# Layer 1's state space steps spread evenly over grouped-query attention in a two-layer hybrid diffusion step

## The chip, the core and the metric

The kernel runs on one core of a Trainium2 chip. The metric is the time of one execution on the device, in microseconds (us); the figure for the kernel before is the median of three runs, 1797.16 us (1796.97 to 1809.3).

## The reference

Two layers of a backbone over 128 prompt tokens and 512 latent tokens, width 1024. Each layer computes, cut to what matters here:

```python
h = layer_norm(x) * (1.0 + sc1) + sh1
z = h @ lp['w_in']
u, q_na, k_na, v_na, q_g, k_g, v_g = jnp.split(z, cuts, axis=-1)
ssm_out, st = ssm_mixer(u, lp, h0_f, h0_b)          # S5: complex diagonal, both directions, then gelu and a gate
na_out  = na_latent(q_na, k_na, v_na, ck, cv, bias)  # 4 heads, 8x16 windows; dense for the prompt
gqa_out = attend_dense(q_g, k_all, v_all)            # 8 query heads on 2 key heads
o = concat([ssm_out, na_out, gqa_out]) @ lp['w_out']
x = layer_norm(ALPHA * x + g1 * o, ...)
```

followed by a SwiGLU feed-forward part. The three mixers read different slices of `z` and do not depend on one another; only `w_out` reads all three. Everything is float32.

## The kernel before

The 640 tokens are five tiles of 128, the first of them the prompt. A product with a weight matrix is split into a high and a low half and takes three matmuls (`mm3`, L311 to L313): high by high, low by high, high by low. The halves of a weight come from a cast on ACT (L283) and a subtraction on POOL or DVE (L284).

A scheduler of the tile framework sets the order on each engine. It takes the program as it is written and weighs it with priorities; units of attention stand under a high priority (`PRIO` = 300), so that what is written between them, the state space steps among it, fills behind them. Each engine then runs its own list strictly in that order. PSUM comes from three pools of two buffers each: `psM` (weights' products, L714, L724, the transposes of L808, the gate of L825), `psT` (transposes and the second products of attention), `psS` (scores, and the second products of the state space model, L767 and L770). Loads and stores are issued by SP, in one list.

`layer` runs, per layer:

1. GQA: keys and values, then 18 units (`pipelined`, one unit ahead). A unit's scores are L1157, its exponentials L1163, its second product L1184. After each unit `between(n)` writes some steps of other work: steps of the state space generator by the table `SSMN`, and by `WINN` pieces of the `w_in` product that neighbourhood attention needs (L311 to L313 with 128x320 results; L1265 copies a piece out of PSUM and L1266 stores it to the scratch `zqk`).
2. NA (neighbourhood attention): two head pairs of five units, one for the prompt and four for the latent tiles. `na_prep` loads `zqk` (L876) and casts it (ACT L877, L878, L283; DVE L879, L284); the prompt's scores are L916; a latent unit's front is L942, L943, L947 into `psS`, then DVE L948 with ACT L950, DVE's maximum L952, ACT's exponentials L955; its back transposes (L859), copies out (ACT L290 or DVE L288), multiplies (L978), divides by the sums (L853, ACT L982, DVE L983) and splits the result (ACT L283, DVE L284). Two fronts run ahead of a back (`DEPTH` = 2). `na_prep` of the second pair is written ahead of its sixth unit (`PREP1`). After the backs, `SSMC` = (1, 2, 0, 2, 1, 0, 1, 0, 2, 1) writes state space steps that are left.
3. `wout`: the product with `w_out`, then the feed-forward part. Its first matmul in layer 1 starts at 1237.04 us.

The state space generator (`ssm`, L671) has 17 steps over eight pairs of groups. Step 1 loads u and writes pair 0's front: loads of four tables (L697, L698, L699, L709) and four matmuls (L714). Step 2p+2 is pair p's turn (four transposes, L724), the next pair's front, and pair p's rotation on DVE (L732 to L753, with a scan in L742). Step 2p+3 is pair p's back (L767, L770, copied out by ACT, L772). Step 17 is the last back and the tail: the state out (L793 to L799), two gelus on ACT (L802, with a table load ahead), 16 transposes (L808), the gate (L825, tanh L827) and the split.

In layer 1 before, 11 of the 17 steps stand in GQA (its eighth to seventeenth units) and six in NA, the tail among them after the back of NA's fifth unit.

Of the kernel before, what the change touches and what calls it, by code (L numbers as in the profile page):

```python
# [157 lines left out]
class Build:  # L158
# [2 lines left out]
    SIZES = dict(b5=1280, xs=640, ys=768, k4=1024, ev=512, zt=512)  # L161
    BUFS = dict(b5=6, xs=8, ys=4, k4=10, ev=4, zt=2)
    TILES = (2, 1, 4, 3, 0)
    SSMN = (0, 0, 0, 0, 0, 0, 0, 1, 1, 1, 1, 1, 1, 1, 1, 1, 2, 0)
    WINN = (2, 0, 1, 1, 2, 0, 1, 1, 1, 1, 1, 1, 1, 1, 1, 1, 0, 2)
    ADAN = (0,) * 6 + (1,) * 6 + (0,) * 6
    FILA = (2, 3, 2, 2, 2)
# [1190 lines left out]
    def layer(self, l, A, xsrc, T, nxt, tab, todo):  # L1358

        nc, I = self.nc, self.I  # L1360
        V, S, G = nc.vector, nc.scalar, nc.gpsimd
        M, zkv = A["M"], A["zkv"]
        hh, hl = A["h"]
        zq, sss, put_q = A["zq"], A["sss"], A["put_q"]
        znv = self.dp.tile([NT, 128, 256], F32, name=self.nm("znv"))
        zu = self.dp.tile([256, NTOK], F32, name=self.nm("zu"))
        zqk = [self.dp.tile([2, 128, NTOK], F32, name=self.nm("zqk")) for _ in range(2)]
        mixd = self.dp.tile([4, 128, NTOK], F32, name=self.nm("mixd"))

        def put_v(i, t, ps):  # L1370
            nc.sync.dma_start(znv[i], t)
            if i == 0:
                nc.sync.dma_start(self.O["na_v"][l], t)

        def tiles(piece, put, order=range(NT)):
            w = self.win_w(l, piece)
            for i in order:
                yield self.win_tile(w, i, hh, hl, put)

        def features(piece, put):  # L1380
            w = self.win_w(l, piece)
            for m in range(2):
                for b in range(2):
                    yield self.win_T(w, m, b, hh, hl, put)

        def chain(*gens):
            for g in gens:
                yield from g

        K = self.gqa_kv(l, zkv)  # L1390
        for _ in features(0, self.put_u(zu)):
            pass
        mx = []

        def mixed(k):

            if not mx:
                mx.extend(self.newh())
            return mx[0][:, k], mx[1][:, k]

        ssm = self.ssm(l, zu, T, mixed)
        fill = chain(tiles(6, put_q(1)), tiles(3, put_v), features(1, self.put_qk(l, 0, zqk[0])),
                     features(2, self.put_qk(l, 1, zqk[1])))
        for _ in range(self.FILL0[l]):
            next(fill, None)
        for _ in range(self.TAB1):
            next(tab, None)
        units, preps = [], []
        for kv in range(2):
            u, prep = self.gqa_units(l, kv, zq[kv], K, sss[kv], mixd)  # L1410
            units += u
            preps += [(prep, a[2][0]) for a in u]

        def between(n):
            for _ in range(self.TABN[n]):
                next(tab, None)
            for _ in range(self.SSMN[n]):
                next(ssm, None)
            for _ in range(self.WINN[n]):
                next(fill, None)  # L1420
            for _ in range(self.ADAN[n]):
                if todo:
                    self.ada(l, M, *todo.pop(0))
            if n + self.AHEAD < len(units):
                with self.tc.high_priority(self.PRIO):
                    preps[n + self.AHEAD][0](preps[n + self.AHEAD][1])

        self.pipelined(units, 1, between)
        for _ in fill:
            pass  # L1430
        Ns = [self.na_prep(l, 0, zqk[0], znv)]

        def gqa_out(k):
            t = self.k4()[:, 0:SLAB]
            nc.sync.dma_start(t, mixd[k])
            self.split(t, *mixed(4 + k), V if self.MIXE[k] else G)

        units = self.na_units(l, Ns[0], *mixed(2))
        live, n, depth = {}, 0, self.DEPTH
        for n in range(10 + depth):  # L1440
            if n == self.PREP1:
                Ns.append(self.na_prep(l, 1, zqk[1], znv))
                units = units + self.na_units(l, Ns[1], *mixed(3))
            if n < 10:
                with self.tc.high_priority(self.PRIO):
                    live[n] = units[n][0](units[n][2])
            for k in range(4):
                if self.MIX[k] == n:
                    gqa_out(k)
            if n >= depth:  # L1450
                with self.tc.high_priority(self.PRIO):
                    units[n - depth][1](units[n - depth][2], live.pop(n - depth))
                for _ in range(self.SSMC[n - depth]):
                    next(ssm, None)
        for _ in ssm:
            pass
        return self.wout(l, M, mx, xsrc, nxt)
# [457 lines left out]
```

## Time and profile before

| | us |
|---|---|
| median of three runs | 1797.16 |
| lowest, highest | 1796.97, 1809.3 |
| the profiled execution | 1788.01 |
| its span in the trace | 1786.0 |
| layer 1, GQA's first scores (L1157) | from 1041.35 |
| layer 1, NA's first scores (L916) | from 1183.93 |
| layer 1, first matmul of `w_out` | from 1237.04 |

The profiled execution is one of its own and took 9.2 us less than the median. Its span leaves out 2.0 us around the program. PE is TensorE, PEld its weight loads, DVE VectorE, ACT ScalarE, POOL GpSimd, SP the engine that issues DMAs. Mean granted TensorE clock over the span is 0.96 of full speed; in a stretch of it that reads 1.0 the clock is at 2.4 GHz, at 0.5 it is at 1.2 GHz, and between them it was at each for a part.

### The profile page before, as it was taken

The page shows a single profiled execution, that of the slowest core. Times are in us where ns is not written, and L with a number is a line of the kernel's source. Part 1 is how long each engine was busy: PE and PEld are TensorE (multiplying, and loading weights), DVE is VectorE, ACT ScalarE, POOL GpSimd, SP SyncE. Part 2 cuts the span into 40 slices and gives each one's busy share as a digit, 9 for nine tenths or more (in the row PEclk, how much of TensorE's full clock was granted, in tenths as well). Part 3 has the DMA queues.
Part 4 walks back from the last instruction along what each step waited for, and adds up shares of the span by engine and source line. Part 5 has one row for each costly group of instructions (what it writes and reads, how often), then busy time and mean ns, then how long its engine had stood idle before and what let it go on. Part 6 is the DMA issues. An engine that isn't in the chain of part 4 may idle for free. (4 is left out here: it accounts for less than half of the span.)

```text
span 1786.0 us, 31489 instructions
## 1 busy us (share of the span) xinstructions
PE 1641.2 (92%) x11624; PEld 1435.8 (80%) x11624; DVE 1222.5 (68%) x2460; ACT 827.3 (46%) x1800; POOL 763.5 (43%) x651
## 2 busy tenths in 40 slices
PE   5899899898899999999897989998979999999997
PEld 2898677676788888798796978876859899998995
DVE  5765546627678776778877565565487687876777
ACT  5444446657443334243345556665574242433433
POOL 3853203059235343346266232111785254454463
PEclk9999899798999999999999999998989999999999
DMA  9445767446353645232324243463542231222212
GB/s 335 112 126 139 238 194 213 123 158 203 107 172 122 195 127 182 81 121 71 121 85 157 92 129 96 111 187 115 180 148 85 94 107 59 92 74 69 98 62 81
DMA packets 183114, 234.90 MB, mean 132 GB/s; under 512 B 78960, under 2 KB 112048, under 8 KB 182960
## 3 DMA queue, kind: packets, MB, share of 16 engines
q1 hardware_dynamic: 182960, 232.88, 42.3%
q8 instruction: 92, 1.51, 0.3%
q14 instruction: 62, 0.51, 0.1%
HBM read 203.57 MB, written 29.39 MB: 130 GB/s over the span
## 5 line engine op out<-in xcount | busy, mean ns | idle before, releaser
L284 POOL TENSOR_TENSOR wl<-wr,wh 128x512 fp32r<-128x512 f32 x362 | 504.2, 1413 | 522.8 <-ACT wh L283 343.2
L283 ACT CAST wh<-wr 128x512 fp32r<-128x512 f32 x450 | 275.2, 619 | 383.9 <-DVE wr L1597 88.6
L311 PE MATMUL psM<-hh,wh 128*128 128x320 f32 x560 | 180.3, 322 | 2.3 <-DVE ys L1647 1.1
L313 PE MATMUL psM<-hh,wl 128*128 128x320 f32 x560 | 177.9, 318 | 0.0
L312 PE MATMUL psM<-hl,wh 128*128 128x320 f32 x560 | 177.8, 318 | 0.0
L311 PEld LDWEIGHTS psM<-hh,wh 128*128 128x128 f32 x560 | 108.5, 194 | 6.2 <-issue 1.8
L311 PE MATMUL psT<-hh,wh 128*128 128x320 f32 x352 | 109.9, 312 | 0.0
L313 PEld LDWEIGHTS psM<-hh,wl 128*128 128x128 f32 x560 | 108.6, 194 | 1.5 <-issue 1.4
L312 PE MATMUL psT<-hl,wh 128*128 128x320 f32 x352 | 109.2, 310 | 0.0
L313 PE MATMUL psT<-hh,wl 128*128 128x320 f32 x352 | 109.0, 310 | 0.0
L312 PEld LDWEIGHTS psM<-hl,wh 128*128 128x128 f32 x560 | 108.7, 194 | 0.3
L230 POOL TENSOR_TENSOR sm<-sm,mhalf 128x1 f32<-128x1 f32 (+2 forms) x46 | 54.3, 1182 | 92.3 <-DVE sm L260 49.3
L1647 DVE TENSOR_TENSOR ys<-ys,psM 128x320 f32<-128x320 f32 x140 | 65.0, 481 | 33.8 <-PE psM L313 31.9
L1160 DVE TENSOR_REDUCE psS<-psS 128x1 f32<-128x640 f32 x64 | 52.7, 828 | 47.4 <-PE psS L1157 45.6
L1647 DVE TENSOR_TENSOR ys<-ys,psT 128x320 f32<-128x320 f32 x140 | 65.0, 481 | 28.8 <-PE psT L313 27.7
L311 PE MATMUL psT<-b,wh 128*128 128x320 f32 x240 | 76.5, 319 | 8.3 <-DVE ys L1647 7.4
L311 PE MATMUL psM<-b,wh 128*128 128x320 f32 x240 | 76.1, 317 | 5.8 <-DVE ys L1647 5.8
L284 POOL TENSOR_TENSOR wl<-ws,wh 128x512 fp32r<-128x512 f32 x40 | 53.6, 1340 | 64.4 <-ACT wh L283 62.6
L859 PE MATMUL psT<-ident,ys 128*128 128x128 f32 x440 | 73.2, 285 | 5.8 <-DVE hl L284 3.3
L311 PE MATMUL psM<-wh,xs 128*128 128x512 f32 x190 | 74.9, 394 | 3.7 <-DVE k L1771 3.5
L311 PE MATMUL psT<-wh,xs 128*128 128x512 f32 x190 | 75.6, 398 | 2.9 <-DVE k L1771 2.9
L1597 DVE TENSOR_TENSOR ws<-wr,wr 128x512 f32<-128x512 f32 x40 | 37.0, 926 | 58.9 <-DMA wr<-in_w_ffn_in_dram 28.3
(440 smaller groups left out, 4907.9 us busy)
## 6 DMA issues: line engine op xcount, KB each, us to landing
wr<-in_w_ffn_in_dram SPq DMA_DIRECT2D x88, 512.0 KB, 3.7
ev<-in_w_ada_dram SPq DMA_DIRECT2D x112, 256.0 KB, 4.0
wr<-in_w_ffn_out_dram SPq DMA_DIRECT2D x40, 512.0 KB, 3.9
wr<-in_w_out_dram SPq DMA_DIRECT2D x32, 512.0 KB, 3.6
wr<-in_w_in_dram SPq DMA_DIRECT2D x28, 512.0 KB, 4.8
wa<-in_w_ada_dram SPq DMA_DIRECT2D x24, 512.0 KB, 4.7
k<-in_x_dram SPq DMA_DIRECT2D x10, 512.0 KB, 5.6
xs<-zqk SPq DMA_DIRECT2D x32, 160.0 KB, 3.7
```

The source lines that it names most:

```text
L230: self.nc.gpsimd.tensor_tensor(out=o, in0=v, in1=self.mhalf.broadcast_to([128, v.shape[1]]), op=ALU.pow)
L283: nc.scalar.copy(hi, src)
L284: (lo_eng or nc.vector).tensor_tensor(out=lo, in0=src, in1=hi.bitcast(F32), op=ALU.subtract)
L311: nc.tensor.matmul(ps, lhsT=ah, rhs=bh, start=first, stop=False)
L312: nc.tensor.matmul(ps, lhsT=ah, rhs=bl, start=False, stop=False)
L313: nc.tensor.matmul(ps, lhsT=al, rhs=bh, start=False, stop=last)
L859: self.nc.tensor.transpose(pt[:, j * 128:(j + 1) * 128], s, self.ident)
L1160: V.tensor_reduce(out=m, in_=sp[:, :, 0:320], axis=AX.XY, op=ALU.max, negate=True)
L1597: V.tensor_tensor(out=o, in0=x, in1=y, op=op)
L1647: V.tensor_tensor(out=o, in0=x, in1=y, op=ALU.add)
```

## The change

The table of steps becomes one row per layer. Layer 0 keeps its row. In layer 1, one step stands after each of the third to seventeenth units, so 15 of 17 steps are written in GQA and two are left for NA: the last pair's turn and rotation stand there after the first back, and the last back with the tail after the second.

```diff
-    SSMN = (0, 0, 0, 0, 0, 0, 0, 1, 1, 1, 1, 1, 1, 1, 1, 1, 2, 0)
+    SSMN = ((0,) * 7 + (1,) * 9 + (2, 0), (0, 0) + (1,) * 15 + (0,))
...
         def between(n):
...
-            for _ in range(self.SSMN[n]):
+            for _ in range(self.SSMN[l][n]):
                 next(ssm, None)
```

No instruction is added or taken away; they move from layer 1's third GQA unit on, up to the start of `w_out`. Three places:

PE where NA begins, before: the back of pair 4 (L767, L770), the last two matmuls of `w_in` (L312, L313), a transpose of `na_prep`, the turn of pair 5 (L724), and the first latent scores (L942).

```order
L767 MATMUL psS_2426_13203<-k4_2386_12942,k4_2387_12943 80x128 x7
L770 MATMUL psS_2426_13203<-k4_2385_12941,k4_2230_12112 80x128 x2
L312 MATMUL psM_2430_13230<-hl_1952_10410,wh_2369_12850 128x320
L313 MATMUL psM_2430_13230<-hh_1951_10409,wl_2370_12851 128x320
L859 MATMUL psT_2443_13293<-ident_84,ev_2440_13286 128x128 x2
L724 MATMUL psM_2462_13368<-ident_84,k4_2424_13173 128x80 x4
L942 MATMUL psS_2453_13320<-b5_2433_13259,b5_2432_13258 128x256
```

PE at the same place, with the change: the back there is pair 6's.

```order
L770 MATMUL psS_2438_13303<-k4_2374_12939,k4_2142_11634 80x128 x2
L311 MATMUL psM_2442_13330<-hh_1951_10409,wh_2379_12973 128x320
L312 MATMUL psM_2442_13330<-hl_1952_10410,wh_2379_12973 128x320
L942 MATMUL psS_2465_13420<-b5_2445_13359,b5_2444_13358 128x256
L942 MATMUL psS_2465_13420<-b5_2446_13360,b5_2444_13358 128x256
L943 MATMUL psS_2465_13420<-mask_150 128x256
L313 MATMUL psM_2442_13330<-hh_1951_10409,wl_2380_12974 128x320
L311 MATMUL psM_2442_13330<-hh_1951_10409,wh_2379_12973 128x320
```

The last piece of `w_in`, which ended before NA's first latent scores, now lies across them: 22 of its 24 matmuls stand behind the first L942, most of them ahead of the second unit's L942. What stood there of pairs 4 and 5 stands in GQA.

ACT behind the first two latent fronts (`ys_2452` and `ys_2456` are their probabilities), before: the exponentials (L955) stand ahead of the second pair's casts (L877, L878).

```order
L950 ACTIVATE ys_2452_13319<-psS_2453_13320 128x2x128
L950 ACTIVATE ys_2456_13339<-psS_2457_13340 128x2x128
L757 COPY fs_2228_12102<-k4_2424_13173 128x2 x2
L955 ACTIVATE ys_2452_13319,sm_2455_13335<-ys_2452_13319,sm_2454_13333 128x384 x2
L955 ACTIVATE ys_2456_13339,sm_2459_13355<-ys_2456_13339,sm_2458_13353 128x384 x2
L950 ACTIVATE ys_2467_13405<-psS_2468_13406 128x2x128
L877 CAST b5_2490_13544<-xs_2493_13547 64x640
L878 CAST b5_2489_13543<-xs_2493_13547 64x640
```

With the change (the fronts are `ys_2464` and `ys_2468`):

```order
L950 ACTIVATE ys_2464_13419<-psS_2465_13420 128x2x128
L950 ACTIVATE ys_2468_13439<-psS_2469_13440 128x2x128
L757 COPY fs_2140_11624<-k4_2423_13187 128x2 x2
L877 CAST b5_2508_13661<-xs_2511_13664 64x640
L878 CAST b5_2507_13660<-xs_2511_13664 64x640
L955 ACTIVATE ys_2464_13419,sm_2467_13435<-ys_2464_13419,sm_2466_13433 128x384 x2
L955 ACTIVATE ys_2468_13439,sm_2471_13455<-ys_2468_13439,sm_2470_13453 128x384 x2
L877 CAST b5_2508_13661<-xs_2513_13675 64x640
L950 ACTIVATE ys_2475_13490<-psS_2476_13491 128x2x128
```

The two casts of `na_prep` of the second pair, which read loads from `zqk`, stand ahead of the exponentials.

ACT around the tail's gelus (L802), before:

```order
L772 COPY k4_2231_12121<-psS_2523_13713 80x2x4x16
L772 COPY k4_2232_12122<-psS_2523_13713 80x2x4x16
L802 ACT_TABLE_LOAD
L802 ACTIVATE k4_2231_12121<-k4_2231_12121 80x1024
L802 ACTIVATE k4_2232_12122<-k4_2232_12122 80x1024
L290 COPY ys_2519_13689<-psT_2520_13690 128x512
L982 COPY zt_2510_13621<-psT_2509_13609 128x128
L955 ACT_TABLE_LOAD
L955 ACTIVATE ys_2513_13661,sm_2516_13677<-ys_2513_13661,sm_2515_13675 128x384 x2
```

With the change:

```order
L878 CAST b5_2507_13660<-xs_2513_13675 64x640
L283 CAST b5_2508_13661<-xs_2510_13663 128x640
L290 COPY ys_2479_13510<-psT_2480_13511 128x512
L802 ACT_TABLE_LOAD
L802 ACTIVATE k4_2143_11643<-k4_2143_11643 80x1024
L802 ACTIVATE k4_2144_11644<-k4_2144_11644 80x1024
L283 CAST b5_2508_13661<-xs_2512_13674 128x640
L950 ACTIVATE ys_2499_13616<-psS_2500_13617 128x2x128
L955 ACT_TABLE_LOAD
L955 ACTIVATE ys_2475_13490,sm_2478_13506<-ys_2475_13490,sm_2477_13504 128x384 x2
```

Before, the gelus come behind the copy of the last back (L772) and their second table load (L955) leads to the exponentials of the sixth latent front (`ys_2513`). With the change they stand behind the casts of the second pair, and their second table load leads to the exponentials of the third front (`ys_2475`).

## Rows read from the trace of the kernel before

**Rows 1.** The page's first part: busy time, share of the span, instructions of each engine

```profile
PE 1641.2 (92%) x11624; PEld 1435.8 (80%) x11624; DVE 1222.5 (68%) x2460; ACT 827.3 (46%) x1800; POOL 763.5 (43%) x651
```

**Rows 2.** Stretches: length, then PE, PEld, DVE, ACT, POOL busy, PEclk, DMA share, GB/s

```profile
1041.00:1110.00 69.00, 63.99 (x570) 57.59 (x571) 41.74 (x104) 43.14 (x107) 16.11 (x18) 0.98 0.34 91
1110.00:1183.90 73.90, 72.64 (x649) 64.87 (x646) 42.27 (x116) 47.77 (x124) 14.03 (x23) 1.00 0.48 131
1183.90:1237.04 53.14, 46.68 (x313) 35.47 (x313) 35.82 (x99) 31.75 (x91) 7.39 (x12) 0.81 0.56 155
1190.00:1200.00 10.00, 8.76 (x45) 6.24 (x46) 6.71 (x16) 5.67 (x17) 0.59 (x3) 0.66 0.89 270
1200.00:1210.00 10.00, 6.87 (x54) 4.96 (x52) 8.70 (x20) 7.24 (x19) 0.74 (x4) 0.99 0.69 135
1210.00:1220.00 10.00, 9.82 (x51) 7.66 (x52) 7.48 (x33) 4.22 (x17) 0.00 (x0) 0.50 0.30 87
1230.00:1240.00 10.00, 8.61 (x47) 6.70 (x43) 5.83 (x14) 5.64 (x20) 3.06 (x2) 0.69 0.41 139
```

**Rows 3.** Waits of PE, 1180 to 1240: in total, times, longest

```profile
PE psS L916 <- ACT b L878: 1.6, 1, 1.6
PE psT L978 <- DVE ys L288: 1.4, 2, 0.9
PE psT L859 <- DVE hl L284: 1.4, 1, 1.4
```

**Rows 4.** Timeline of PE, 1184 to 1204: start, us, line, count, [idle before]

```profile
1184.55 1.10 PE L767 MATMUL psS<-k,k 64*80 64x128 f32 x14
1185.58 0.66 PE L770 MATMUL psS<-k,k 128*80 128x128 f32 x4
...
1186.60 0.44 PE L724 MATMUL psM<-ident,k 80*128 80x80 f32 x4
...
1192.20 0.50 PE L942 MATMUL psS<-b,b 128*128 128x256 f32 x2 [1.24 <-ACT ys L950]
...
1203.46 1.06 PE L714 MATMUL psM<-k,k 128*80 128x256 f32 x4 [0.67 <-DMA k<-tabV]
```

**Rows 5.** Timeline of PE, first and nineteenth of the last `w_in` matmuls

```profile
1180.54 0.31 PE L313 MATMUL psM<-hh,wl 128*128 128x320 f32 x1
...
1183.17 0.31 PE L313 MATMUL psM<-hh,wl 128*128 128x320 f32 x1
```

**Rows 6.** Timeline of PE, 1195 to 1200: a front and a back in a slow stretch

```profile
1195.23 1.91 PE L714 MATMUL psM<-k,k 128*80 128x256 f32 x4
1197.07 2.00 PE L767 MATMUL psS<-k,k 64*80 64x128 f32 x16
1199.00 0.94 PE L770 MATMUL psS<-k,k 128*80 128x128 f32 x4
```

**Rows 7.** Timeline of ACT in NA: first exponential, a cast of the second pair, gelus, table loads

```profile
1194.85 0.62 ACT L955 ACTIVATE ys<-ys,sm 128x384 f32<-128x384 f32 x1 [0.86 <-DVE sm L952]
...
1198.47 0.72 ACT L877 CAST b<-xs 64x640 fp32r<-64x640 f32 x1 [0.85 <-DMA xs<-zqk]
...
1223.63 1.28 ACT L802 ACT_TABLE_LOAD   x1
1224.93 2.00 ACT L802 ACTIVATE k<-k 80x1024 f32<-80x1024 f32 x2
...
1227.58 1.28 ACT L955 ACT_TABLE_LOAD   x1
```

**Rows 8.** Timeline of SP at the second pair's `zqk`

```profile
1187.95 0.34 SPq L1266 DMA_DIRECT2D zqk<-zt  x1
...
1193.49 4.29 SPq L876 DMA_DIRECT2D xs<-zqk  x7
```

**Rows 9.** Timeline of DVE, first and last operation of pair 6's rotation

```profile
1203.15 0.87 DVE L732 TENSOR_TENSOR xs<-psM,k 128x316 f32<-128x316 f32 x2
...
1210.58 0.68 DVE L753 TENSOR_TENSOR k<-xs 128x80 f32<-128x80 f32 x4
```

## The prediction

> **What bounds the kernel now.** I read the share of busy time first: PE is busy for 92% of the span, every other engine for at most 68% [rows 1]. So time is lost where PE idles or runs at its lower clock, and I looked at both by stretches around the change [rows 2]. In layer 1's GQA, from 1110 us to the start of NA, PE is busy 72.64 of 73.90 us at a granted clock of 1.00; that stretch already carries eleven state space steps, and there is no room in it for more PE work. From 1041 to 1110, PE is idle for 69.00 - 63.99 = 5.01 us. NA, up to the first matmul of `w_out`, takes 53.14 us, of which PE idles 53.14 - 46.68 = 6.46 us, and its mean clock is 0.81. The ten-microsecond rows say where the clock goes: 0.66, 0.50 and 0.69 in three of them, so some (0.34 + 0.50 + 0.31) x 10 = 11.5 us of work at the full level were not done there. The row from 1200 to 1210, with the engine idle 3.13 us, still has 0.99, and the half level (1.2 GHz) fills the row behind it. NA thus loses about 18 us, and this is the most that the change can win; it is 1.0% of 1797.
>
> The waits of PE in NA are few: 1.6 us for ACT's cast L878, 1.4 us (twice, together) for DVE's copy L288, 1.4 us for DVE's split behind L859 [rows 3], 1.24 us for ACT's L950 before the third latent front, 0.67 us for the load of pair 7's table [rows 4]. Together 6.3 us, nearly all of the 6.46.
>
> **The change part by part.** *Two pairs leave NA for GQA.* Fronts 6 and 7, turns 5 and 6, backs 4 (its rest) and 5 stand in GQA with the change; the count of operations is two pairs. A pair costs PE by durations at the full level 1.06 (L714) + 0.44 (L724) + 1.10 x 16/14 = 1.26 (L767) + 0.66 (L770) = 3.4 us [rows 4]; a duration overlaps the next by 0.1 to 0.2, so I take 2.8. GQA gets 2 x 2.8 = 5.6 us more of work on an engine that is full there.
>
> *A piece of `w_in` slides the other way.* 22 of its matmuls, a step each of (1183.17 - 1180.54)/18 = 0.146 us [rows 5], are 3.2 us, and the order also puts GQA's last second product and one prompt back behind NA's first scores; I take 2 us for these, an estimate from some 30 small matmuls at 0.07. So 5.3 us go from GQA into NA, and NA's start stays where it is within a microsecond: 5.6 - 5.3 = +0.3. The stretches' bounds: if the five idle microseconds from 1041 to 1110 took the first steps, -2; if steps that wait for ACT or DVE stop PE there, +2. I take 0.
>
> *Work in NA.* It loses 5.6 and gets 5.3 us: 0 with the GQA term. The gate's matmuls (L825) come ahead of `w_out`'s first, and the last latent front goes behind it; both only change place on PE.
>
> *Clock.* Of the two pairs that leave, a front and a back stood in a half-level stretch: L714 took 1.91 there, L767 2.00, L770 0.94 [rows 6] against 1.06, 1.26 and 0.66. That is 0.85 + 0.74 + 0.28 = 1.9 us, and the back of pair 6 in the row of 0.50 was as slow, 1.0 more. The `w_in` work that comes in stands behind GQA's dense end, at the full level. I take -3.0 us. Bounds: 0, if other work fills the slow stretches, and -11.5, if none is left.
>
> *Idle, five places.* (1) The third latent front needs a PSUM buffer that L948 and L950 free, and DVE's rotation stands ahead of L948. Before, PE has the first two latent fronts between the turn (L724, 1186.60) and this wait: 5.6 us to 1192.20 [rows 4]. With the change the turn of pair 7 stands behind their first parts, so 1.6 us less cover: 1.2 becomes 2.8, +1.6. (2) The load of a table for the last front, 0.67 us, goes: -0.7. (3) The waits for L878 and for L288 stay, +0: the casts come earlier in ACT's list but their loads later. (4) The gelus. ACT's list carries a table load, two gelus and a table load, 1.28 + 2.00 + 1.28 = 4.56 us [rows 7]; before, PE has three and more latent fronts and transposes meanwhile; with the change the exponentials of the third front, the copies (L982) and splits (L283) of the first backs stand behind the gelus, and one front and some transposes are all that covers. The wait at L859 goes from 1.4 to 3.4 us, +2.0. (5) The last latent front waits for an L950 that now stands behind the tanhs (L827) and the table load for `w_out`'s side work, a new wait: one front's ACT chain less its cover, 2.3 us, an estimate from the 1.28 us load and an operation or two of 0.4 to 0.7. Sum 1.6 - 0.7 + 0 + 2.0 + 2.3 = +5.2 us. Bounds: -6.3, if every wait of NA goes, and +13, below.
>
> *SP and POOL.* The table loads of pairs 6 and 7 leave the middle of the second pair's `zqk` loads. That helps little, since those wait for the store: L1266 at 1187.95, the first loads at 1193.49, the cast at 1198.47 [rows 7, 8], 10.5 us after the store. The store follows the last piece of `w_in`, which slides 4 us and more into NA, and the casts go with it. The scratch and the tables of the first pairs are long written when GQA's third unit starts, so no load holds the earlier steps. Near the end of `w_out` a weight load that waits for POOL stands ahead of loads that stood ahead of it; the last load needed is unchanged: 0, bounds -4 and +4. DVE gets two rotations in GQA; one is spread over 1211.26 - 1203.15 = 8.1 us in NA with other work between [rows 9], so two are 16 us at most, against 27 us that DVE idles from 1041 to 1110 [rows 2]: covered. Without that cover they would push 2 or 3 units' chains by a rotation's piece, some 2 us in all, which is the GQA bound above.
>
> *Sum.* 0 (places of work) - 3.0 (clock) + 5.2 (idle) = +2.2 us, say +2. On the profiled execution, 1788.01, that gives 1790; this execution ran 9.2 us under the median of the runs, and the change falls on the same stage in each, so 1797.2 + 2 = **1799 us**.
>
> *What the Trainium skill adds.* In the trace each of the two table loads at the gelus takes 1.28 us, and the gelus start 0.02 us after the first ends (1223.63 + 1.28 = 1224.91, 1224.93) [rows 7]. The Trainium skill ("ScalarE: Activation LUTs", section "What ACT_TABLE_LOAD costs") gives the same load and a drain of about 1.38 us on top of it for each switch. By that page the two switches would cost 2 x 1.38 = 2.8 us more of ACT time in the new place, and the sum would be near +5; the trace of before shows no such gap here, so I keep the rows.
>
> **The rivals.** *NA is relieved.* DVE is busy 8.70 of 10 us while two rotations stand among NA's work [rows 2]; one of them lies from 1203.15 to 1211.26 [rows 9]. With one rotation left, the waits for L288 and L878 and the table's go (1.4 + 1.6 + 0.7 = 3.7 us), and without that idle the half-level row behind it goes (5.0 us): -8.7, or 1788. For it: those waits and that row stand exactly where the rotations stand. Against it: the casts wait for a load, not for DVE, and ACT gets a new queue.
>
> *ACT becomes NA's bound (slower).* The first exponentials now stand behind two casts that need the second pair's loads. Store to cast took 10.5 us [rows 7, 8]; the store moves from 4 us behind NA's start to 8, the cast to 18.5, while the exponentials started at 1194.85 before [rows 7], 10.9 us in, and could start some 2 us later with `w_in`'s piece ahead of them and pair 4's back gone, at 13. So 5.5 us of delay, all of which PE sees if it runs out of fronts and of pair 7's back in between, plus the +5.2 above and a slow stretch more: 5.5 + 5.2 + 1 = +11.7, or 1809. It decides from the point where the loads land later than PE's work ahead of the first backs lasts; each microsecond behind that is a microsecond of the total. For it: the order on ACT. Against it: that PE has 5.3 us of `w_in` behind NA's start which it had not before.
>
> *GQA has slack for the steps.* PE's row may hide room: weight loads are busy 64.87 of 73.90 us there, 88% [rows 2]. If the moved pairs ran in that slack, the 5.6 us would be free and the total -5.6 + 2 = -3.4, or 1794. Against it: the `w_in` matmuls step by 0.146 us without a gap [rows 5], at the full level, and the idle is 1.26 us. The Trainium skill ("Perfetto Trace Analysis", section "Identifying the Most-Contended Engine") holds matmul busy time for a bad measure and the share of weight loads for a good one, and would thus give this rival more weight than the rows do.
>
> *The change does nothing*, as the work only changes place and the waits change partners: 0, or 1797; it reads like the forecast.
>
> **How the numbers follow.** The forecast (with the case of nothing) 0.58, relieved 0.20, ACT's bound 0.17, slack 0.05. The forecast's own range is its value and 4 us to both sides of it, from the wait terms: 1795 to 1803. To leave out no more than 2 in 10 it must reach to the relieved case and to ACT's bound with its own spread: 1786 to 1811. A measurement of this kernel can tell about 1%, 18 us, from no change. Faster by over 1% needs more than all that NA loses: 0.04. Slower by over 1% needs ACT's bound and 6 us more, such as a further stretch at the half level: 0.07. Within 1%: 0.89.
>
> **What would show it.** In the profile after: GQA from 1110 on is still full, and the first L916 is within 1 us of 1183.9 plus or minus 2; the load wait at L714 is gone from NA; PE waits at the third front for L950 near 2.8 us, behind the gelus near 3.4 us, and at the last front for L950 near 2.3 us; two half-level stretches stay; the first `w_out` matmul is at 1237 to 1241 with the gate's matmuls ahead of it. The forecast is wrong if NA's idle falls under 4 us (relieved), if L955's first operation starts later than 20 us after the first L916 and PE idles before the first back (ACT's bound), or if L916 comes 4 us earlier (slack).

## The result and the profile after

The changed kernel took 1809.67 us, median of 19 runs, beside 1797.16 us of the kernel before. The ratio is 1.0061 with a 95% interval of 1.0043 to 1.0078: 11 us slower (7.7 to 14.0). That is under 1% and clear of zero. The two medians are 12.5 us apart; this document goes by the ratios, which leave out two slow runs, one of this kernel (3114.6 us) and one of e_pool below (1816.57 us).

Its profiled execution took 1806.14 us, with a span of 1804.1 us:

```profile
span 1804.1 us, 31491 instructions
PE 1643.4 (91%) x11624; PEld 1436.9 (80%) x11624; DVE 1223.2 (68%) x2460; ACT 826.5 (46%) x1800; POOL 763.8 (42%) x651
```

PE is busy for 2 us more than in [rows 1], and the span is 18.1 us longer. Not all of that is the change: layer 1's first GQA scores start at 1046.43 instead of 1041.35 us, and up to there no instruction was moved. So I compare stages from that landmark on. The stretches that answer to [rows 2], cut at the same instructions (first L1157, first L916, first matmul of `w_out`), with the same columns:

```profile
1046.43:1115.00 68.57, 60.81 (x528) 52.83 (x529) 42.34 (x110) 39.38 (x106) 13.69 (x21) 0.95 0.43 109
1115.00:1196.07 81.07, 78.81 (x693) 70.37 (x691) 48.22 (x135) 51.16 (x133) 14.95 (x24) 1.00 0.46 121
1196.07:1253.80 57.73, 50.70 (x309) 38.85 (x308) 28.83 (x70) 35.31 (x84) 10.86 (x9) 0.76 0.49 154
1206.00:1216.00 10.00, 8.05 (x41) 5.99 (x41) 8.43 (x22) 3.25 (x12) 1.99 (x3) 0.65 0.84 257
1216.00:1226.00 10.00, 9.35 (x62) 7.62 (x58) 4.98 (x12) 9.92 (x20) 0.00 (x0) 0.67 0.21 56
1226.00:1236.00 10.00, 7.79 (x40) 5.43 (x39) 6.72 (x18) 6.71 (x21) 0.00 (x0) 0.67 0.27 69
1236.00:1246.00 10.00, 10.00 (x48) 7.01 (x48) 2.00 (x5) 3.96 (x8) 1.53 (x1) 0.81 0.36 116
1246.00:1256.00 10.00, 7.78 (x46) 5.53 (x43) 4.80 (x10) 9.42 (x21) 5.13 (x4) 0.70 0.89 313
```

GQA takes 149.64 us where it took 142.58, NA 57.73 where it took 53.11, and from there to the end it is 550.3 against 549.0. The cut at `w_out` does not part the same work, though: before, the gate's 16 matmuls (L825) stand behind it and every latent front ahead of it; with the change it is the gate that stands ahead (7.1 us of PE's time) and the last front behind. Up to the 193rd matmul of `w_out` both kernels have done the same of these, first the kernel before, then the changed one:

```profile
1183.93:1294.16 110.23, 103.77 (x606) 80.69 (x605) 58.24 (x147) 63.13 (x153) 40.68 (x37) 0.89 0.53 164
1196.07:1311.05 114.98, 107.95 (x604) 84.21 (x604) 50.37 (x121) 62.16 (x144) 41.56 (x33) 0.85 0.47 151
```

That is 4.8 us more, with 0.6 us more idle and a lower mean clock.

In GQA PE is busy 139.62 us against 136.63 and idle 10.0 against 6.0. Some of this comes ahead of the first instruction that was moved (L714 at 1061.10). At GQA's second scores PE waits, first before and then with the change:

```profile
1045.39 0.94 PE L1157 MATMUL psS<-b,xs 128*128 128x320 f32 x4 [2.32 <-ACT ys L1163]
1051.53 1.43 PE L1157 MATMUL psS<-b,xs 128*128 128x320 f32 x4 [3.39 <-ACT ys L1163]
```

Up to the last instruction before the moved ones it is 13.1 us before and 14.6 with the change; over all kernels below it is 13.1 to 16.8, also where nothing in GQA was changed. In NA the idle grows by only 0.6 us (57.73 - 50.70 = 7.03), but the mean clock falls from 0.81 to 0.76: the half level (1.2 GHz) fills a good part of every ten microseconds from 1206 to 1256.

The waits of PE in NA, to be held against [rows 3]:

```profile
PE psT L859 <- ACT ys L290: 3.5, 2, 2.1
PE psS L942 <- ACT ys L950: 1.7, 3, 0.7
PE psS L947 <- DVE xs L897: 1.3, 1, 1.3
PE psT L978 <- DVE ys L288: 0.5, 1, 0.5
```

The wait at L859 is 3.5 us in two pieces, now behind ACT's copy L290; the longer one, behind the gelus, is this:

```profile
1229.83 0.69 PE L859 MATMUL psT<-ident,ys 128*128 128x128 f32 x2 [2.15 <-ACT ys L290]
```

The waits for L878 [rows 3] and for the last pair's table [rows 4] are gone.

ACT in NA, the rows that answer to [rows 7]:

```profile
1215.26 0.72 ACT L877 CAST b<-xs 64x640 fp32r<-64x640 f32 x1 [2.84 <-DMA xs<-zqk]
1216.00 0.72 ACT L878 CAST b<-xs 64x640 fp32r<-64x640 f32 x1
1216.63 0.61 ACT L955 ACTIVATE ys<-ys,sm 128x384 f32<-128x384 f32 x1
...
1221.74 0.58 ACT L290 COPY ys<-psT 128x512 f32<-128x512 f32 x1
1222.34 1.28 ACT L802 ACT_TABLE_LOAD   x1
1223.63 2.00 ACT L802 ACTIVATE k<-k 80x1024 f32<-80x1024 f32 x2
...
1226.55 1.28 ACT L955 ACT_TABLE_LOAD   x1
1227.84 0.61 ACT L955 ACTIVATE ys<-ys,sm 128x384 f32<-128x384 f32 x1
...
1229.20 0.58 ACT L290 COPY ys<-psT 128x512 f32<-128x512 f32 x1
```

ACT stood idle 2.84 us for the load of `zqk` and did the cast L877 and L878 before the first exponential (L955), which starts 20.6 us behind the first L916; it was 10.9 before. Then come the gelus with their table loads: 4.2 us between the start of the first load and that of the second. The copies of the transposes (L290 at 1221.74 and 1229.20) stand on both sides of them, and PE's 2.15 us wait at L859 ends with the second of them.

And three waits of PE in GQA that the kernel before does not have, from the timeline of PE:

```profile
1101.36 1.09 PE L714 MATMUL psM<-k,k 128*80 128x256 f32 x4 [1.14 <-ACT sm L1227]
...
1130.71 0.85 PE L1157 MATMUL psS<-b,xs 128*128 128x320 f32 x4 [1.23 <-ACT ys L1163]
...
1191.33 0.41 PE L311 MATMUL psM<-hh,wh 128*128 128x320 f32 x1 [1.03 <-ACT fs L735]
```

A front waits for ACT to copy a tile of the `w_in` product out of a `psM` buffer; scores wait for exponentials that are late on ACT; and a `w_in` product waits for ACT's L735 to leave the buffer that holds a turn, behind four casts of NA's first pair (L877 and L878, 1188.19 to 1191.04). ACT is not where the first two begin:

```profile
1100.93 0.37 ACT L1227 COPY sm<-psM 128x256 f32<-128x256 f32 x1 [2.04 <-DMA out_na_v_dram<-sm]
...
1124.13 0.42 SPq L1079 DMA_DIRECT2D xs<-zq  x1
...
1129.08 0.50 DVE L1081 TENSOR_TENSOR xs<-xs,k 128x256 f32<-128x256 f32 x1 [1.94 <-DMA xs<-zq]
...
1129.68 0.88 ACT L1163 ACTIVATE ys<-psS,sm,sm 128x640 f32<-128x640 f32 x1 [1.42 <-DVE sm L1161]
```

The copy L1227 itself waited for a store of a tile to end. The exponentials waited for DVE's L1161, which stands behind L1081 on DVE, and that waited for a load of queries (`zq`). SP issued this load at 1124.13, directly behind three table loads of a pair (L697 to L699, from 1122.70). Over GQA these two waits grow, first before and then with the change:

```profile
DVE xs L1081 <- DMA xs<-zq: 0.6, 1, 0.6
ACT ys L1163 <- DVE sm L1161: 8.1, 6, 2.8
DVE xs L1081 <- DMA xs<-zq: 4.9, 4, 1.9
ACT ys L1163 <- DVE sm L1161: 14.6, 9, 3.7
```

### The profile page after: what moved, and what is told of

Read it like the earlier page. It is cut to its first block, busy times and chain, and to the rows that moved or that the text cites. A ratio compares the mean times of both kernels' runs of the same rounds, so it can differ in the third digit from the quotient of the medians.

```text
span 1804.1 us, 31491 instructions
## 1 busy us (share of the span) xinstructions
PE 1643.4 (91%) x11624; PEld 1436.9 (80%) x11624; DVE 1223.2 (68%) x2460; ACT 826.5 (46%) x1800; POOL 763.8 (42%) x651
## 4 chain that ended last, share of the span: by engine, by line
PE 59%; DVE 12%; DMA 11%; POOL 7%; issue 6%; ACT 4%; SPq 1%; POOLq 0%; DVEq 0%; ACTq 0%
PE psM L311 9%; PE psM L313 8%; PE psM L312 8%; PE psT L311 6%; PE psT L312 5%; PE psT L313 5%; POOL wl L284 4%; DMA ev<-in_w_ada_dram 3%; PE psT L859 3%; PE psS L1157 2%; DMA wr<-in_w_ffn_in_dram 2%; PE psT L1184 2%; DVE wr L1597 1%; DVE ev L615 1%; DVE k L1298 1%
## 5 line engine op out<-in xcount | busy, mean ns | idle before, releaser
L313 PE MATMUL psM<-hh,wl 128*128 128x320 f32 x560 | 176.8, 316 | 0.0
L312 PE MATMUL psM<-hl,wh 128*128 128x320 f32 x560 | 176.5, 315 | 0.0
L312 PE MATMUL psT<-hl,wh 128*128 128x320 f32 x352 | 109.5, 311 | 0.0
L313 PE MATMUL psT<-hh,wl 128*128 128x320 f32 x352 | 109.3, 311 | 0.0
L313 PEld LDWEIGHTS psM<-hh,wl 128*128 128x128 f32 x560 | 107.5, 192 | 1.6 <-issue 1.4
L312 PEld LDWEIGHTS psM<-hl,wh 128*128 128x128 f32 x560 | 107.6, 192 | 0.3
L859 PE MATMUL psT<-ident,ys 128*128 128x128 f32 x440 | 75.5, 290 | 6.7 <-ACT ys L290 4.5
```

Source lines behind the costliest of these rows:

```text
L312: nc.tensor.matmul(ps, lhsT=ah, rhs=bl, start=False, stop=False)
L313: nc.tensor.matmul(ps, lhsT=al, rhs=bh, start=False, stop=last)
L859: self.nc.tensor.transpose(pt[:, j * 128:(j + 1) * 128], s, self.ident)
```

## The experiments

Three theories stood at the start: the loss is in NA, on ACT (A); it is in GQA, where two more pairs stall the chain (B); it is the last piece of `w_in` that slides into NA (C). Twelve kernels were run, 6 to 12 executions of each, beside the kernel before. This table gives the ratio of the times and, from each kernel's one profiled execution, the lengths of the stages between the same landmarks, in us. The last column is from GQA's first scores to the end of the span.

| kernel | ratio, 95% interval | GQA | NA | rest | sum |
|---|---|---|---|---|---|
| before | 1 | 142.6 | 53.1 | 549.0 | 744.7 |
| the change | 1.0061 (1.0043 to 1.0078) | 149.6 | 57.7 | 550.3 | 757.7 |
| e_tail5 | 1.0036 (1.0016 to 1.0055) | 149.2 | 58.6 | 539.9 | 747.7 |
| e_early11 | 1.0042 (1.0019 to 1.0065) | 146.7 | 56.0 | 548.9 | 751.6 |
| e_win | 1.0109 (1.0079 to 1.0138) | 159.4 | 53.4 | 547.6 | 760.4 |
| e_both | 1.0064 (1.0046 to 1.0082) | 158.4 | 44.8 | 550.7 | 753.9 |
| e_tanh | 1.0028 (1.0004 to 1.0053) | 148.8 | 50.6 | 550.1 | 749.5 |
| e_late15t5 | 1.0057 (1.0029 to 1.0085) | 156.9 | 54.1 | 543.4 | 754.4 |
| e_13t5 | 1.0029 (1.0007 to 1.0051) | 147.7 | 57.7 | 548.7 | 754.1 |
| e_btail2 | 1.0067 (1.0039 to 1.0095) | 144.1 | 70.1 | 544.7 | 758.9 |
| e_poolafter | 1.0054 (1.0032 to 1.0076) | 150.1 | 49.7 | 547.8 | 747.6 |
| e_pool | 1.0020 (0.9997 to 1.0042) | 148.8 | 52.0 | 547.0 | 747.9 |
| e_btanh | 0.9986 (0.9964 to 1.0009) | 142.4 | 50.6 | 547.3 | 740.2 |
| e_btail9 | 1.0007 (0.9982 to 1.0031) | 142.4 | 49.4 | 552.6 | 744.5 |

The profile of one execution can stand some us off its kernel's median (e_poolafter's sum is 10 us under the change's, its ratio only 0.0007 under), so the ratios decide on totals, and the stages only where several kernels with the same order there agree. NA and rest are to be compared only where the same work stands ahead of `w_out`: in the kernel before, e_early11, e_btail2, e_btanh and e_btail9 the whole gate stands behind the cut, in the change, e_win, e_tanh and e_poolafter ahead of it, in the other five kernels one half on each side.

Where GQA's order is that of before (before, e_btail2, e_btanh, e_btail9), it takes 142.4 to 144.1 us; where it is that of the change (the change, e_tail5, e_tanh, e_poolafter, e_pool), 148.8 to 150.1. These two groups do not touch; their means differ by 6.4 us. Counted from the last instruction ahead of the first moved one, which leaves out the wait that differs anyway, they are 129.1 to 129.5 and 134.3 to 136.9: 5.8 us apart, 3.1 of it PE's busy time and 2.7 idle. The granted clock is 1.00 there in all of them but e_poolafter (0.99), so this price is not one of the clock.

**The tail behind the fifth unit** (e_tail5).

```diff
-    SSMC = (1, 2, 0, 2, 1, 0, 1, 0, 2, 1)
+    SSMC = ((1, 2, 0, 2, 1, 0, 1, 0, 2, 1), (1, 0, 0, 0, 1, 0, 0, 0, 0, 0))
...
-                for _ in range(self.SSMC[n - depth]):
+                for _ in range(self.SSMC[l][n - depth]):
```

> The changed kernel, with the last back and the tail (gelus, table loads, gate) put back behind the fifth unit of neighbourhood attention (NA) in layer 1; the other 16 steps as in the change. Theory A (ACT binds NA: casts of the second head pair ahead of the first exponentials, then the early gelus with their table loads): the gelu half of the loss comes back, about 3 to 5 of the 11 us that the change costs, so 6 to 8 us over the kernel before. Theory B (the loss is in grouped-query attention (GQA), where the two more pairs stall its chain): nothing comes back, 10 to 12 us over. Theory C (the loss is the last piece of w_in and the loads behind it, alone): also 10 to 12.

Ratio 1.0036, 6.5 us over (2.9 to 9.9): in A's range, and under the 10 to 12 of B and C. 4.5 us are back. The difference to the change, 0.0025, has an interval of about 0.0027 to both sides (the two intervals' halves in quadrature), so this run alone does not settle it.

**The same eleven steps, five units earlier** (e_early11).

```diff
-    SSMN = ((0,) * 7 + (1,) * 9 + (2, 0), (0, 0) + (1,) * 15 + (0,))
+    SSMN = ((0,) * 7 + (1,) * 9 + (2, 0), (0, 0, 1, 1, 1, 1, 1, 1, 1, 1, 1, 1, 1, 0, 0, 0, 0, 0))
```

> The table of the kernel before moved five units forward in layer 1: 11 steps after GQA's third to thirteenth units, six left for NA as before. No pair changes its stage, and the last w_in piece ends before NA's first scores. Theory A (ACT in NA): no loss, within 3 us of the kernel before. Theory B (early steps stall GQA): most of the loss stays, 6 to 11 us over. Theory C (w_in slides into NA): no loss, within 3 us.

Ratio 1.0042, 7.5 us over: as B said, but the profile says it of other places than B did. GQA grows by 4.1 us, of which the turn of pair 5 and the back of pair 4 that now end before NA are a part, and 1.2 us stand ahead of its first moved instruction. NA grows by 2.9; it has that turn and back less, and GQA's last second product more. The timeline of ACT at NA's start in this run:

```profile
1209.77 0.37 ACT L896 CAST xs<-psT 128x256 fp32r<-128x256 f32 x1
1214.02 0.72 ACT L877 CAST b<-xs 64x640 fp32r<-64x640 f32 x1 [3.88 <-DMA xs<-zqk]
...
1215.39 0.36 ACT L926 COPY ys<-psT 128x256 f32<-128x256 f32 x1
...
1218.95 0.61 ACT L955 ACTIVATE ys<-ys,sm 128x384 f32<-128x384 f32 x1
```

And in its timeline of PE the wait that came of it:

```profile
1215.81 0.69 PE L928 MATMUL psT<-ys,k 128*64 128x128 f32 x4 [3.04 <-ACT ys L926]
```

The casts of the second pair again stand ahead of the fronts' work on ACT: 3.88 us for the load, and PE waits 3.04 us for the copy L926 behind them. So the order on ACT moves with any shift of the steps, and this run does not separate an early start from that.

**`w_in` earlier** (e_win), **and the tail late as well** (e_both, with the edit of e_tail5 on top).

```diff
-    WINN = (2, 0, 1, 1, 2, 0, 1, 1, 1, 1, 1, 1, 1, 1, 1, 1, 0, 2)
+    WINN = ((2, 0, 1, 1, 2, 0, 1, 1, 1, 1, 1, 1, 1, 1, 1, 1, 0, 2), (2, 0, 1, 1, 2, 1, 1, 1, 2, 1, 1, 1, 1, 1, 1, 1, 0, 0))
...
-            for _ in range(self.WINN[n]):
+            for _ in range(self.WINN[l][n]):
```

> The changed kernel, with layer 1's w_in pieces for NA written earlier (one each after GQA's sixth, ninth and later units, none after the last two), so that the last piece, its stores and the loads for NA's second head pair end before NA's first scores and its casts no longer stand ahead of the first exponentials. The gelus stay early. Theory A: the casts' half comes back, 4 to 6 us; left 5 to 7 over the kernel before. Theory B: nothing comes back, 10 to 12 over, or more, since GQA is fuller. Theory C: all comes back, within 3 us of the kernel before.

> w_in pieces earlier as in the run before this one, and the tail behind NA's fifth unit: two pairs have left NA, and neither the casts nor the gelus stand in the way. Theory A: the whole loss comes back and NA is relieved of two rotations: 0 to 8 us under the kernel before. Theory B: 8 to 12 us over it, as the loss is in GQA. Theory C: within 3 us of it, like the run with w_in alone.

Ratios 1.0109 and 1.0064, 20 and 11.5 us over: C falls, and with the sign turned. A's numbers (5 to 7 over, and 0 to 8 under) are missed as well, and B's (10 to 12 or more, and 8 to 12) hold. GQA takes 159.4 us, 9.8 more than with the change, for some 5 us of work that came back into it. The largest wait of PE that is new in that GQA says where a part of the rest is:

```profile
PE psM L724 <- ACT k L716: 2.6, 1, 2.6
```

It stands at GQA's end: with no `w_in` matmuls left to put ahead of it, the last pair's turn waits for ACT's copy. The piece that slid into NA was no obstacle but cover. With casts and tail both out of the way, and two pairs gone with nothing in their place (e_both), NA shrinks to 44.8 us, 8.3 under before, which GQA more than takes back. The late tail is worth 0.0045 between these two, 8 us, with some 6 to both sides.

**No table loads** (e_tanh on the change, e_btanh on the kernel before).

```diff
-            S.activation(ysb[hf][0:NJ], ysb[hf][0:NJ], AF.Gelu_apprx_tanh)
+            S.activation(ysb[hf][0:NJ], ysb[hf][0:NJ], (AF.Tanh if l else AF.Gelu_apprx_tanh))
```

> The changed kernel with tanh in place of layer 1's gelu (L802): same shapes, same place, same order on every engine, but no table load ahead of it and none behind it, since the exponentials' table holds tanh. The output is not the reference's: layer 1's gelu is left out. Theory D1 (the early tail costs by its two table loads, 2.56 us of ACT's queue): 2 to 5 us under the changed kernel, so 6 to 9 over the kernel before. Theory D2 (the early tail costs by its place: the last back, transposes and gate ahead of NA's units): nothing comes back, 10 to 12 over.

> The kernel before with tanh in place of layer 1's gelu (no table loads there; layer 1's gelu is left out, so the output is not the reference's). In the changed kernel the same edit took 6 us away. Theory D1' (the loads cost by their place, and at the fifth unit PE has fronts to do meanwhile): 0 to 3 us under the kernel before. Theory D1'' (the loads cost the same anywhere): 5 to 7 under, and the early tail's price would then have another cause.

Ratios 1.0028 and 0.9986. On the change the edit takes 0.0033 away, 6 us, with an interval of about 0.0030 to both sides: just clear of zero. On the kernel before it takes 2.5 us (6.5 under to 1.6 over), not clear of zero. NA's stretch in the profile of e_tanh:

```profile
1191.04:1241.66 50.62, 44.57 (x308) 34.98 (x308) 28.68 (x70) 32.66 (x82) 10.86 (x9) 0.86 0.58 176
```

And in that of e_btanh:

```profile
1183.70:1234.28 50.58, 45.21 (x313) 34.36 (x312) 34.81 (x97) 28.95 (x89) 7.36 (x12) 0.83 0.59 162
```

Both are 50.6 us long. With the table loads it is 57.7 after and 53.1 before. By the ratios, D1's sign holds with a number just above its 2 to 5 us, D2 (nothing comes back) falls narrowly, and D1' has its 0 to 3. That the same 2.56 us of loads cost more behind the second unit than behind the fifth is what the two numbers say, but their difference, 3.4 us, is not clear of zero, and the interval on the kernel before reaches into D1'' (5 to 7 under). It is not shown.

**The number of steps in GQA and their start** (e_13t5, e_late15t5; `SSMC` of layer 1 is (1, 1, 1, 0, 1, 0, 0, 0, 0, 0) in the first and that of e_tail5 in the second, so the tail is behind NA's fifth unit in both).

```diff
-    SSMN = ((0,) * 7 + (1,) * 9 + (2, 0), (0, 0) + (1,) * 15 + (0,))
+    SSMN = ((0,) * 7 + (1,) * 9 + (2, 0), (0, 0, 0, 0, 1, 1, 1, 1, 1, 1, 1, 1, 1, 1, 1, 1, 1, 0))
...
+    SSMN = ((0,) * 7 + (1,) * 9 + (2, 0), (0, 0, 0, 0, 0, 0, 0, 1, 2, 1, 2, 1, 2, 1, 2, 1, 2, 0))
```

> 13 steps in GQA, one after each of its fifth to seventeenth units, the tail behind NA's fifth unit: one pair moved, and a start half way between the kernel before and the change. Theory B1: 2 to 5 us over the kernel before. Theory B2: 2 to 5 us over. A value at or over 6.5 (that of the run with 15 steps) would say that neither the start nor the count sets the loss, but the piece of w_in that all of these push behind NA's first scores.

> 15 steps in GQA as in the change, but from the eighth unit on, one and two in turn, and the tail behind NA's fifth unit. Its partner is the run with 15 steps from the third unit on and the same tail (6.5 us over the kernel before by its ratio). Theory B1 (steps that start early stall GQA): 0 to 3 us over. Theory B2 (two more pairs in GQA stall it, whenever they stand there): 5 to 8 us over.

Ratios 1.0029 and 1.0057. A late start does not help, so B1 falls; 10 us over is more than B2's 5 to 8, though its interval (5 to 15 us) takes that range in. With one pair moved (e_13t5) the loss is 5.2 us, just above the 2 to 5 of both theories and about what two cost with the same tail (6.5): the ratios do not show the dose. GQA's length does: counted from the same instruction as above, it is 130.9 us with one pair, beside 129.1 to 129.5 with none and 134.3 to 136.9 with two, and the piece of `w_in` that slides into NA is the same in both.

**An early tail in the kernel before** (e_btail2: `SSMC` of layer 1 is (3, 3, 0, 0, 0, 0, 0, 0, 0, 0), the steps in GQA as before).

> The kernel before (11 steps in GQA), with the six steps that are left for NA written three after its first and three after its second unit, so the tail comes as early as in the change. Theory D (an early tail costs, by itself): 4 to 8 us over the kernel before. If the early tail costs only together with the late casts of the second head pair: 0 to 3 us over.

Ratio 1.0067, 12 us over (7 to 17): the sign of D and more than its 4 to 8. But its NA of 70.1 us lost its time elsewhere:

```profile
PE psS L767 <- DVE k L753: 4.4, 1, 4.4
PE psT L859 <- DVE k L753: 3.5, 1, 3.5
PE psM L714 <- DMA k<-tabV: 3.0, 1, 3.0
```

10.9 us of PE waiting for bunched rotations and a table's load. The run says that six steps behind two units are too many, and nothing clean of the gelus.

**The casts on POOL** (e_poolafter on the change, e_pool on e_tail5).

```diff
-            S.copy(kh[X], qr[X])
-            S.copy(t[R], qr[R])
+            (G.tensor_copy if l and hp else S.copy)(kh[X], qr[X])
+            (G.tensor_copy if l and hp else S.copy)(t[R], qr[R])
```

> The changed kernel with the two casts per head (L877, L878) of layer 1's second head pair on POOL, so that nothing on ACT waits for the zqk loads ahead of the first exponentials; the early gelus stay. Theory E (the casts ahead of the exponentials are a part of the loss): 2 to 5 us under the changed kernel, 6 to 9 over the kernel before. Without E (they only fill a wait that DVE's maxima set): 10 to 12 over.

> The same casts on POOL, and the tail behind NA's fifth unit: casts and gelus are both out of the way, and what is left is the two pairs in GQA. Theory E with the GQA part (about 5 us): 1 to 5 us over the kernel before. Without E: 5 to 8 over, as the run with the late tail alone (6.5).

Ratios 1.0054 and 1.0020: 1.3 and 2.9 us back. Both have the sign of E, and neither is clear of zero; the first, 9.7 us over, is nearer to the 10 to 12 without E than to E's 6 to 9, the second, 3.6, is in the range with E. With both obstacles out of ACT's way (e_pool), 0.0041 of the loss is back, with about 0.0028 to both sides, so the two together are clear. What is left is 3.6 us (-0.5 to 7.5), and its stages:

```profile
1050.33:1199.13 148.80, 139.63 (x1218) 123.01 (x1218) 91.19 (x243) 90.62 (x238) 28.78 (x45) 0.99 0.44 116
1199.13:1251.17 52.04, 48.41 (x317) 37.88 (x316) 29.72 (x73) 29.50 (x81) 11.05 (x11) 0.77 0.51 150
```

GQA is as long as with the change. NA and rest together are 599.0 us against 602.1 before: with the work that left them they are some 3 us shorter, and that is why GQA's longer stage is not the whole loss.

**The tail behind the tenth unit, in the kernel before** (e_btail9: layer 1's `SSMC` is (1, 2, 0, 2, 0, 0, 0, 0, 0, 1)).

> The kernel before with layer 1's tail behind NA's tenth unit in place of the fifth: gelus and table loads behind most of NA's exponentials, the gate later in w_out. If the loads' place sets their price and w_out's first half (GQA's rows) covers the gate: 1 to 5 us under the kernel before. If the place no longer matters that late, or the gate holds w_out up: 0 to 4 over.

Ratio 1.0007 (0.9982 to 1.0031): NA 3.7 us shorter, the rest 3.6 us longer. The tail's 16 transposes (L808) now stand behind the cut with the gate, which is a part of both. The two expectations are not told apart. No version that was run beats the kernel before beyond its interval.

## Why the prediction was right and where it was wrong

The time lies in the stated range (1786 to 1811) and within 1%, and it is slower, as forecast. But 11 us are not the +2 of the sum, and 1809.67 is beyond the forecast's own 1795 to 1803: the range holds because it reached to the rival "ACT becomes NA's bound", at 1809. That the time falls on this rival's number is luck. The rival's 5.5 us for the casts are not seen on PE, and a loss in GQA, which the sum put at 0, stands in their place. The sign, too, did not come about as it was added up: idle +5.2 against clock -3.0 was measured as some +0.6 and a clock that costs time.

- *Places of work, "0", with GQA's bounds -2 and +2.* This step failed. GQA takes 6.4 us more, in five profiles against four, or 5.8 behind the wait that differs anyway. PE is busy 2.9 us more there (139.62 against 136.63 with the change; 139.10 to 140.89 and 136.47 to 136.58 in the others) where the two pairs less the `w_in` piece were to make 0.3. With 5.3 us taken out (3.2 and 2, so rather 5.2), that is 8.2 us for two pairs: some 4.1 each, an estimate, not the 2.8 that I took from start to start, nor the 3.4 of the durations. NA has two pairs less in return, which is how 5.8 us in GQA go with the 3.6 us (-0.5 to 7.5) that e_pool leaves.
- *The rest of GQA's growth is idle*, 2.7 us, against "covered" for DVE's rotations and "no load holds the earlier steps". I looked at the loads that the steps need; the steps' own table loads stand in SP's list ahead of the units' query loads, DVE waits for these 4.9 us instead of 0.6, and the exponentials and PE come behind it. In the four other kernels with the change's order DVE's wait for `zq` is 3.8 to 4.7 us, in the three with that of before 0.4 to 2.1. A front and a `w_in` product wait besides for `psM` buffers that ACT has not copied out. That these waits are what the idle is made of is read from the rows; no run took one of them away.
- *What bounds the kernel.* Of the eleven steps in GQA before, the first two begin ahead of 1110 (L714 at 1088.36, L724 at 1099.01), so the full stretch does not carry all eleven; the conclusion that it has no room stands.
- *The slide of `w_in`.* It happened as the order showed. That it was harmless to NA is right (e_win), and the reason is stronger than I gave: GQA's last units need it behind them to have something to do.
- *Clock, -3.0.* Wrong in sign. NA's mean clock fell from 0.81 to 0.76; (1 - 0.76) x 57.73 - (1 - 0.81) x 53.14 = 3.8 us more were lost. Over the 18 runs of the changed kernel the mean clock of the span is 0.953, over 91 runs of the kernel before beside the later kernels 0.955 to 0.956: 84 us not done at the full level against 78 to 81, 3.5 to 6 us more. The slow stretches did not leave with the work that had stood in them; what came in ran slowly in its turn.
- *Idle, +5.2.* Measured +0.6 in NA. Item by item: the third front's wait is 0.65 us instead of 2.8 (wrong); the table's load is gone (right); the waits for L878 and L288, which were to stay, fell from 3.0 us to 0.5 (wrong); L859's is 3.5 against 3.4 (right in size: 2.15 us behind the gelus, and 1.33 us later where the split was); the last front, behind `w_out`'s first matmuls, shows no wait instead of 2.3 us (wrong); a wait for DVE's L897 of 1.3 us at the first L947 was not foreseen.
- *The gelus, +2.0.* Mis-sized. The late tail gives back 4.5 of the 11 us, with 4.7 to both sides; between e_win and e_both it gives 8, and the loads alone, taken away in e_tanh, 6. All three have one sign, and the last two are clear of zero. As L859's wait is about what I forecast, the rest is not idle there. Over its 12 runs e_tanh has a mean clock of 0.956, beside 0.953 with the change, so a part of it is the clock; how the loads bring that about is open.
- *The casts, in the rival, 5.5 us.* The order did what the rival said: the first cast starts 19.2 us behind the first L916 (18.5 in the rival) and the first exponential 20.6. But DVE's maxima (L952) were late by themselves, so without the casts the exponentials would have started at 17.2 and not at 13. With the casts on POOL (e_poolafter, first L916 at 1202.68) they do. First DVE's maximum with the change, then the exponential in e_poolafter:

```profile
1212.31 0.94 DVE L952 TENSOR_REDUCE sm<-ys 128x2 f32<-128x768 f32 x1
...
1219.89 0.62 ACT L955 ACTIVATE ys<-ys,sm 128x384 f32<-128x384 f32 x1 [0.87 <-DVE sm L952]
```

  So the casts held the exponentials up by 3.4 us. PE does not idle for it, since pair 7's back stands in between:

```profile
1215.08 2.00 PE L767 MATMUL psS<-k,k 64*80 64x128 f32 x16
1217.01 1.14 PE L770 MATMUL psS<-k,k 128*80 128x128 f32 x4
1217.94 1.49 PE L859 MATMUL psT<-ident,ys 128*128 128x128 f32 x6
```

  The sign that was named for this rival thus came by half: L955 starts later than 20 us, and PE does not idle before the first back. The two runs with the casts on POOL give 1.3 and 2.9 us, neither clear of zero.
- *Relieved, slack, nothing.* NA's stage did not shorten, GQA grew by the moved work and more, and 11 us are clear of nothing. All three fell. On ACT's table switch the trace after again shows the gelu 0.01 us behind the load's end (1222.34 + 1.28) and the load 0.02 us behind the copy ahead of it (1221.74 + 0.58), so the drain of 1.38 us that the Trainium skill gives ("ScalarE: Activation LUTs", section "What ACT_TABLE_LOAD costs") is not seen here.

By the ratios the 11.0 us are thus 4.5 (the early tail), 2.9 (the casts) and 3.6 (what is left, the two pairs in GQA), each with some 4 or 5 us to both sides; the first two together are clear of zero. That the early tail costs and that GQA is longer with the pairs in it is shown by several kernels each; the share of the casts is not shown, and what an early start costs by itself stays open.

## What to carry to other kernels

Work that is moved into a stage whose bounding engine is full is paid there: here two pairs made GQA 5.8 us longer although a piece of other work had left it. Cost it from the stage's busy time and not from the gaps between its instructions, and look at what it brings along: its loads in the list of the DMA issues, ahead of loads that the stage waits for, and the buffers that it shares. When a scheduler sets the order, a shift of background steps also reorders what stands ahead of the critical operations on the in-order engines; read those lists around the first dependent operation, look for operations there that wait for a load or load a table, and then look whether the bounding engine has work meanwhile. The casts held the exponentials up by 3.4 us and PE did not idle; behind the gelus it did, for 2.15 us. Before two stages are compared, look whether the same work stands between the cuts.

## What the runs showed that was not expected

Between profiled executions, layer 1's first GQA scores start anywhere from 1041.35 (before, e_btanh) to 1052.61 us (e_poolafter), with the same instructions in the same order up to there. A comparison of whole spans of two single executions carries up to 11 us of this, as much as the change itself; the lengths of stages between landmarks agree far better (GQA within 1.7 us in each group).

How much of NA runs at the half level differs much between kernels whose order there is the same or nearly so. The mean clock is 0.76 with the change, 0.86 without the table loads (e_tanh), and 0.93 in e_poolafter, which has both loads:

```profile
1202.68:1252.35 49.67, 41.63 (x308) 32.56 (x308) 29.21 (x69) 30.99 (x78) 12.84 (x12) 0.93 0.53 164
```

PE idles there for 8.0 us, 1.0 more than with the change, and NA is 8.1 us shorter, while the ratio says 1.3 us. This execution has the highest mean clock of that kernel's nine (0.962, the lowest being 0.951). So 7.1 us less of NA in the one profile of e_tanh are no measure of what two loads of 1.28 us cost; the 6 us of its ratio are.
